# The first output tile inside the last attention block, and every gate in the blocks

## The chip, the cores and the metric

The kernel runs on one core of a Trainium2 chip. The metric is the device time of one execution in microseconds (us). The engines are named as in the profile: PE is TensorE (matmuls; PEld is its weight load), DVE VectorE, ACT ScalarE, POOL GpSimd, SP SyncE, whose queue issues the DMAs.

## What is computed

A backbone of two layers over 256 context and 2048 latent tokens, width 1024, in fp32. Each layer norms and projects its input once, runs four branches on the projection, multiplies each with SiLU of its own gate z, and projects the four branches together into the residual:

```python
for i in range(DEPTH):
    hl = rms_norm(xl, norm_g[i]) * (1.0 + sc_l[:, None]) + sh_l[:, None]
    (aq_l, ak_l, av_l, az_l, bq_l, bk_l, bv_l, bz_l, cu_l, cv_l, cz_l,
     dq_l, dk_l, dv_l, dz_l, drf_l, drb_l) = split_cols(hl @ w_in[i])
    ...
    y_l = jnp.concatenate([ya_l * jax.nn.silu(az_l), yb_l * jax.nn.silu(bz_l),
                           yc_l * jax.nn.silu(cz_l), yd_l * jax.nn.silu(dz_l)], axis=-1)
    xl = xl + gt_l[:, None] * (y_l @ w_out[i])
return rms_norm(xl, final_norm_g)
```

Branch A is differential attention (4 heads, two softmax maps each, the second subtracted with a learned weight), B grouped-query attention (4 query heads, 2 key heads), C a spatial-gating MLP over chunks of 128 tokens, D gated linear attention scanned in both directions. Latent tokens attend to context and latent tokens; context tokens, in layer 0 alone, to context only.

## The kernel before, in words

A layer has three stages. `proj_attn` and `proj_cd` norm the input, project it for the four branches and run C and D; the normed input goes to DRAM as `hs`, since the gates are projected later. `attention` runs A and B. `output` gates, turns and projects the branches.

**Attention** (L783) has four rounds, one per head, of eight blocks of 256 queries against all 2304 keys, from the last queries to the first; in layer 0 one block of the 256 context queries stands ahead of each round. PE's order is written out by hand: `Slots` (`S.at(slot, function, priority)`) collects calls and runs them slot by slot, by priority within one. A block has 18 slots: 12 score chunks of branch A (`da_chunk`, L893, read by DVE at L898), 6 of branch B for the row maxima (`g_chunk`, L931, L936). The two query transposes (`qb`, L945) close them. After that come, while the next block's chunks run, nine times four transposes of branch A's weights (`tr`, L953, copied by ACT, L957), nine times four score matmuls of branch B turned round (`gs`, L965 and L966, exp on ACT at L968, summed on POOL at L974), the products with V in 64-column tiles (`pvm`, L985) in four groups of 2, 2, 2 and 3 steps, and the output's turn and store (`o1` to `o3`, L992 to L1014). ACT takes the exps of branch A (L907), DVE joins the two maps (`da_comb`, L923). Only PE's order is fixed; a scheduler orders the other engines by data, buffers and the order of writing.

**The gates** (`gates`, L1142) are 24 matmuls for each of 4 groups and each token tile: 72 units in layer 0 (1728 matmuls), 64 in layer 1 (1536). They read `hs` back in halves of 512 KB (`fh`, three buffers), the weights `fw`, and go over PSUM bank `pz` and ACT (L1149) to DRAM as `z`. `Pace.fill` pours them in, at two calls per slot: `EARLY` puts more of them first, and `keep` holds back `HEAD` = 10 units for the start of the output. The last block's tail (its work after its query transposes, with no next block beside it) has `TAIL` = 22 slots of calls.

**The output** (`output`, L1161) goes over the token tiles. For each it steps the backward state of D's scan (`scan`: load of `bst` L1199, steps on DVE L1208, expansion to `SXb` on POOL L494), loads the branches and z (`load`, L1221 to L1225), gates and norms them (`mixers`: Silu L1231, state product `pd` L1235, Square L1242 and the inverse root L166, L167 with a table load, L152), transposes the tile (`turned`: L1257, copied by ACT and DVE) and projects it in two halves of 512 columns (`project`: 24 matmuls L139 to L141 into `po`). Each half of the output weights is loaded in eight pieces (L124) over four `wst` buffers and split into a high and a low part by ACT (L127, L130) and DVE (L128, L131). At the start the kept gates stand between these steps (`pace.units`).

## Time and profile before

| | |
|---|---|
| median of three runs | 4014.12 us (4008.24 to 4018.21) |
| profiled execution, its time | 4011.71 us |
| its span | 4009.9 us |
| mean granted PE clock | 0.974 |
| PE busy | 3724.8 us (93%) in 25908 matmuls |
| weight loads on PE (PEld) | 3068.2 us (77%) |
| DVE / ACT / POOL busy | 2706.0 / 2200.6 / 1182.5 us |

Busy PE time is the time covered by matmul records; neighbouring records overlap, since matmuls are pipelined. A stage is cut out of the span by its first and last instruction: layer 0's attention starts at 667.6 us and layer 1's at 2667.6; the block intervals begin with the first full block's `qb` and end with the last one's; the tail is the last block's rest, and the head lasts from there to the first output matmul (L139).

### The profile page before, as it was taken

How to read it: one execution, taken by the hardware profiler on the slowest of the kernel's cores; microseconds unless marked ns; L12 is line 12 of the kernel's file. 1: busy time of each engine (PE TensorE's matmuls, PEld its weight loads, DVE VectorE, ACT ScalarE, POOL GpSimd, SP SyncE). 2: the span in 40 equal slices, each digit the busy share in tenths (PEclk: the TensorE clock that was granted, in tenths of full speed). 3: DMA queues.
4: the chain of work that ended last, by engine and by line, in shares of the span. 5: the costliest groups of instructions: out<-in, count | busy, mean ns of one | idle time of the engine just before them, and what ended most of it. 6: DMA issues, size and time to landing. Idle time of an engine off the chain costs nothing.

```text
span 4009.9 us, 71922 instructions
## 1 busy us (share of the span) xinstructions
PE 3724.8 (93%) x25908; PEld 3068.2 (77%) x25908; DVE 2706.0 (67%) x6272; ACT 2200.6 (55%) x4527; POOL 1182.5 (29%) x1326
## 2 busy tenths in 40 slices
PE   7999997899999999978989999979999999999698
PEld 5888886787887877767778878867777777777576
DVE  5654443788888888854556544448888888886476
ACT  4433443666666666653444334436676666666464
POOL 1223221233333333332321222213333333334132
PEclk8999998999999999989999999989999999999899
DMA  7654434524234233246556542244242332322743
GB/s 271 194 184 161 147 125 144 157 83 128 86 100 131 85 102 94 86 151 232 177 181 213 170 149 88 89 144 129 80 124 81 114 95 80 99 87 71 249 165 120
DMA packets 407524, 537.73 MB, mean 134 GB/s; under 512 B 107832, under 2 KB 271616, under 8 KB 407168
## 3 DMA queue, kind: packets, MB, share of 16 engines
q1 hardware_dynamic: 407168, 533.14, 41.8%
q8 instruction: 205, 3.36, 0.3%
q14 instruction: 151, 1.24, 0.1%
HBM read 395.63 MB, written 137.32 MB: 133 GB/s over the span
## 4 chain that ended last, share of the span: by engine, by line
PE 34%; DVE 11%; DMA 4%; issue 3%; ACT 2%; POOL 1%; SPq 1%; DVEq 0%; POOLq 0%; ACTq 0%
PE pv L985 4%; DVE e L923 3%; PE pz L1142 3%; DVE junk L936 3%; PE s L893 2%; PE po L139 2%; DVE e L898 2%; PE po L141 2%; PE po L140 2%; PE b L953 2%; DMA fh<-hs 2%; PE s L931 1%; PE b L966 1%; PE b L965 1%; PE pc L139 1%
## 5 line engine op out<-in xcount | busy, mean ns | idle before, releaser
L974 POOL TENSOR_TENSOR acc<-acc,gp 128x512 f32<-128x512 f32 x448 | 591.2, 1320 | 1030.6 <-ACT gp L968 1026.9
L1142 PE MATMUL pz<-fw,fh 128*128 128x256 f32 x3264 | 726.0, 307 | 91.6 <-DMA fh<-hs 70.7
L907 ACT ACTIVATE e<-e,dm 128x1152 f32<-128x1152 f32 x512 | 640.5, 1254 | 17.5 <-DVE e L898 16.7
L1142 PEld LDWEIGHTS pz<-fw,fh 128*128 128x128 f32 x3264 | 543.6, 199 | 108.6 <-issue 34.5
L985 PE MATMUL pv<-gp,v 128*64 128x256 f32 x2320 | 558.4, 386 | 0.0
L985 PE MATMUL pv<-wt,v 128*64 128x256 f32 x2320 | 558.4, 385 | 0.0
L898 DVE TENSOR_SCALAR_CACHE_REDUCE e<-s,dm 128x768 f32<-128x768 f32 x512 | 511.3, 1013 | 47.0 <-PE s L893 41.2
L957 ACT COPY wt<-b 128x512 f32<-128x512 f32 x580 | 338.2, 583 | 364.0 <-PE b L953 361.5
L893 PE MATMUL s<-dak,daq 128*128 128x384 f32 (+1 forms) x1568 | 417.8, 348 | 58.7 <-DVE e L898 34.8
L968 ACT ACTIVATE gp<-b 128x512 f32<-128x512 f32 x580 | 346.2, 597 | 226.5 <-PE b L966 217.8
L923 DVE SCALAR_TENSOR_TENSOR e<-e,r,e 128x576 f32<-128x576 f32 x512 | 459.6, 934 | 2.7
L985 PEld LDWEIGHTS pv<-gp,v 128*64 128x64 f32 x2320 | 296.8, 137 | 162.2 <-issue 13.5
L953 PE MATMUL b<-ident,e 128*128 128x128 f32 x2304 | 360.4, 279 | 9.1 <-ACT wt L957 2.9
L898 DVE TENSOR_SCALAR_CACHE_REDUCE e<-s 128x768 f32<-128x768 f32 x256 | 239.8, 951 | 186.2 <-PE s L893 182.4
L953 PEld LDWEIGHTS b<-ident,e 128*128 128x128 f32 x2304 | 261.2, 140 | 106.3 <-issue 70.4
L936 DVE TENSOR_SCALAR_CACHE_REDUCE junk<-s,gm 128x768 bf16<-128x768 f32 x256 | 259.6, 1014 | 80.2 <-PE s L931 69.6
L965 PE MATMUL b<-qa,ka 128*128 128x256 f32 x1160 | 304.4, 285 | 7.2 <-ACT gp L968 5.5
L893 PEld LDWEIGHTS s<-dak,daq 128*128 128x128 f32 x1568 | 245.6, 193 | 79.5 <-DVE e L898 50.2
L966 PE MATMUL b<-qb,kb 128*128 128x256 f32 x1160 | 301.5, 282 | 0.0
L985 PEld LDWEIGHTS pv<-wt,v 128*64 128x64 f32 x2320 | 296.5, 137 | 0.0
L931 PE MATMUL s<-ka,qa 128*128 128x384 f32 (+1 forms) x784 | 219.0, 360 | 31.0 <-DVE e L898 20.7
L965 PEld LDWEIGHTS b<-qa,ka 128*128 128x128 f32 x1160 | 219.1, 189 | 13.7 <-ACT gp L968 10.8
(276 smaller groups left out, 8087.8 us busy)
## 6 DMA issues: line engine op xcount, KB each, us to landing
fh<-hs SPq DMA_DIRECT2D x272, 512.0 KB
hs<-hh SPq DMA_DIRECT2D x36, 512.0 KB
hs<-hl SPq DMA_DIRECT2D x36, 512.0 KB
hh<-hs SPq DMA_DIRECT2D x36, 512.0 KB
hl<-hs SPq DMA_DIRECT2D x36, 512.0 KB
dak<-aqk SPq DMA_DIRECT2D x96, 192.0 KB
daq<-aqk SPq DMA_DIRECT2D x136, 128.0 KB
z<-zs SPq DMA_DIRECT2D x136, 128.0 KB
```

What stands on the lines that cost most here:

```text
L893: nc.tensor.matmul(s[:, u, :hc], lhsT=Q["daq"][m][:, qt * P : (qt + 1) * P], rhs=R["dak"][m][c][:, u * hc : (u + 1) * hc], start=True, sto ...
L898: nc.vector.tensor_scalar(out=E[qt, m][:, c * ch : (c + 1) * ch].rearrange("p (u f) -> p u f", u=2), in0=s[:, :, :hc], scalar1=-SC, scalar ...
L907: nc.scalar.activation(e, e, AF.Exp, bias=NM[qt, m], scale=-1.0, accum_out=L[qt][:, b, m : m + 1])
L923: nc.vector.scalar_tensor_tensor(out=E0[:, a : a + w], in0=E1[:, a : a + w], scalar=RR[qt][:, 3:4], in1=E0[:, a : a + w], op0=ALU.mult, op ...
L936: nc.vector.tensor_scalar(out=junk[:, :ch].rearrange("p (u f) -> p u f", u=2), in0=s[:, :, :hc], scalar1=-1.0, scalar2=GM.get(qt, BIG), op ...
L953: nc.tensor.transpose(s[:, j * 256 + qt * P : j * 256 + (qt + 1) * P], W[qt][:, k * P : (k + 1) * P], ident)
L965: nc.tensor.matmul(o, lhsT=R["KA"][k // 6][:, ks], rhs=Q["QA"], start=True, stop=False)
L966: nc.tensor.matmul(o, lhsT=R["KB"][k // 6][:, ks], rhs=Q["QB"], start=False, stop=True)
L968: nc.scalar.activation(g, s, AF.Exp, scale=0.125)
L974: nc.gpsimd.tensor_tensor(out=B["acc"], in0=B["acc"], in1=g, op=ALU.add)
L985: nc.tensor.matmul(B["pv"][o : o + 64, :256], lhsT=R["V"][k // VH][:, k % VH, o : o + 64], rhs=x[:, js], start=k == 0, stop=k == nkt - 1,)
L1142: nc.tensor.matmul(ps[:, :256], lhsT=h[:, a, k % 4], rhs=w[:, b], start=k == 0 and z == 0, stop=k == KT - 1 and z == 2)
```

## The change

**The gates** are spread evenly over the calls of the 32 blocks, `EARLY`, `HEAD` and the tail's calls are gone; what is left after the last block's calls is drained before the tail. The first four slots take none.

**The output** becomes a generator whose first part runs as steps in the tail of the last block: at slot 2 the state, the first tile's loads and the first half of the output weights (eight pieces into the free buffers of branch A's weights, `room`), at slot 9 `mixers`, at slot 19 `turned`, from slot 20.5 eight steps of three output matmuls into the gates' bank. PSUM and SBUF tiles for it are lent by attention (`front`). After attention come the second tile's load and scan, the second half of the weights, and the steps tile by tile.

**Context blocks** are laid beside the first full block of a round, a chunk every second slot, with query and row buffers of their own and one exp of 256 in place of two of 128. In layer 0's first round the first full block's query is loaded first, then all keys of branch A, and the context's query after the first keys of branch B and the gates' first weights.

**V products** come in three groups of three steps, a slot earlier after their last step; `da_comb` gets slots of its own.

```diff
-EARLY, HEAD = 1.5, 10
...
-        w = lambda z: z + EARLY * min(z, 40)
-        want = (self.n - self.keep) * min(1, w(self.seen) / w(self.calls))
+        want = self.n * self.seen / self.calls
...
-    def units(self, n):
-        for _ in range(n):
-            while self.step():
-                pass
+    def drain(self):
+        for _ in self.steps:
+            pass
...
+        if isinstance(stage, bass.AP):
+            st = stage
+        else:
+            pool, tag, bufs = stage or (self.xp, "wst", self.wst)
+            st = pool.tile([P, 512 if stage is None else w], F32, name=tag, tag=tag, bufs=bufs)
...
-                gate = self.attention(i)
+                out = self.output(i)
+                self.attention(i, out)
                 self.xp, self.wst = dense.enter_context(self.pool(f"dn{i}", 2)), 4
-                ahead = self.output(i, *gate)
+                for _ in out:
+                    pass
+                ahead = self.ahead
...
+                ctx = "c" if q0 == 0 else ""
+                bufs = 1 if q0 == 0 else 3
...
-                    w = nk // 2
+                    w = nk // 2 if full else nk
...
-                s = base
+
+                s, step = (base, 1) if full else (base + 0.25, 2)
+                combs = ((11, 12, 14, 16.5), (17.5, 19, 21, 22.5))
                 for qt in range(2):
                     for c in range(nch):
                         for m in range(2):
                             S.at(s, lambda qt=qt, m=m, c=c: da_chunk(qt, m, c), 7)
-                            s += 1 if full else 0.5
+                            s += step
                     for m in range(2):
-                        for b in range(2):
+                        for b in range(2 if full else 1):
                             S.at(s + 1 + 2 * m + b, lambda qt=qt, m=m, b=b: da_exp(qt, m, b), -1)
                     npt = 4 if full else 1
                     for p in range(npt):
-                        S.at(s + 5 + p, lambda qt=qt, p=p: da_comb(qt, p, npt), 0.5)
+                        S.at(base + combs[qt][p] if full else s + 5, lambda qt=qt, p=p: da_comb(qt, p, npt), 0.5)
                 for c in range(nch):
                     for qt in range(2):
                         S.at(s, lambda qt=qt, c=c: g_chunk(qt, c), 0)
-                        s += 1 if full else 0.5
-                S.at(s + full, qb, 8 if full else 2)
-                for z in range(int(base), int(s) + (TAIL if (h, q0) == (3, NCTX) else 0)):
-                    S.at(z, lambda z=z: pace.fill(z), 3)
-                    S.at(z, lambda z=z: pace.fill(z + 0.5), 9)
+                        s += step
...
+                S.at(s + 1, qb, 8)
                 b0 = s + 2
                 if full:
+                    for z in range(base, s):
+                        S.at(z, lambda z=z: pace.fill(z), 3)
+                        S.at(z, lambda z=z: pace.fill(z + 0.5), 9)
                     for u in range(nu):
                         S.at(b0 + 2 * u, lambda u=u: tr(u), 1)
                         S.at(b0 + 2 * u + 1, lambda u=u: gs(u), 4)
-                    for us in ((0, 1), (2, 3), (4, 5), (6, 7, 8)):
+                    for us in ((0, 1, 2), (3, 4, 5), (6, 7, 8)):
+                        e = b0 + 2 * us[-1] + 4.5
                         for u in us:
                             for j in range(2):
-                                S.at(b0 + 2 * us[-1] + 5.5, lambda u=u, j=j: pvm(u, j), 5)
-                    e = b0 + 2 * (nu - 1) + 5.5
+                                S.at(e, lambda u=u, j=j: pvm(u, j), 5)
                 else:
-                    S.at(b0 + 20, lambda: tr(0), 3)
-                    S.at(b0 + 20, lambda: gs(0), 4)
+
+                    e = base + 24.25
+                    S.at(e - 3, lambda: tr(0), 3)
+                    S.at(e - 3, lambda: gs(0), 4)
                     for j in range(2):
-                        S.at(b0 + 20 + 1.5 + j * 0.5, lambda j=j: pvm(0, j), 5)
-                    e = b0 + 20 + 1.5 + 0.5
+                        S.at(e, lambda j=j: pvm(0, j), 5)
                 S.at(e, o1, 5.5)
                 S.at(e + 4, o2, 5)
                 S.at(e + 4, o3, 5.2)
                 return s
...
-            blocks = []
-            for r in range(4):
-                if with_ctx:
-                    blocks.append((r, 0, NCTX))
-                for b in reversed(range(8)):
-                    blocks.append((r, NCTX + 256 * b, NT))
+            blocks = [(r, NCTX + 256 * b) for r in range(4) for b in reversed(range(8))]
             units = 4 * (NTILE if with_ctx else NTILE - CTILE)
-            pace = Pace(self.gates(i, fp, pz), 24 * units, 2 * (32 * 18 + with_ctx * 12 + TAIL), 24 * HEAD)
+            pace = Pace(self.gates(i, fp, pz), 24 * units, 2 * 32 * 18)
             base = 0
             R = new_round(0, None)
-            ld_dak(R, 0)
             Qs = {0: qload(R, blocks[0][1])}
-            if with_ctx:
-                ld_ka(R, 0)
-                Qs[1] = qload(R, blocks[1][1])
+            for c in range(NCH):
+                ld_dak(R, c)
+            ld_ka(R, 0)
+            pace.begin()
             for c in range(1, NCH):
-                ld_dak(R, c)
-            pace.begin()
-            for c in range(with_ctx, NCH):
                 ld_ka(R, c)
             for c in range(2):
                 S.at(6 + 4 * c, lambda c=c, R=R: ld_v(R, c), 8)
-            for bi, (r, q0, nk) in enumerate(blocks):
-                end = block(R, Qs[bi], q0, nk, base)
+            for bi, (r, q0) in enumerate(blocks):
+                if with_ctx and bi % 8 == 0:
+                    block(R, qload(R, 0), 0, NCTX, base)
+                end = block(R, Qs[bi], q0, NT, base)
                 Rx = R
                 if bi + 1 < len(blocks):
                     if blocks[bi + 1][0] != r:
...
                     def pre(bi=bi, Rx=Rx):
                         Qs[bi + 1] = qload(Rx, blocks[bi + 1][1])
 
-                    if bi + 1 not in Qs:
-                        S.at(base + 1, pre, 8)
+                    S.at(base + 1, pre, 8)
...
+            pace.drain()
             dcx.close()
+            zcx.close()
+
+            S.run(base + 2)
+            self.front = dict(
+                pcx=pcx,
+                psum=lambda: pf.tile([P, 2, 512], F32, name="s", tag="s"),
+                bank=lambda: pz.tile([P, 512], F32, name="pz", tag="pz"),
+                room=[ep.tile([P, NT], F32, name=n, tag=n, bufs=b) for n, b in (("e0", 4), ("e0", 4), ("e1", 2))],
+                junk=lambda: tp.tile([P, 512], F32, name="wt", tag="wt", bufs=6),
+            )
+            for slot in (2, 9, 19) + tuple(20.5 + 0.5 * z for z in range(8)):
+                S.at(base + slot, lambda: next(out), 6)
             S.run()
-        return pace, zcx, pcx
...
-                y = self.xp.tile([P, DM], F32, name="xa", tag="xa", bufs=3)
+                if front:
+                    y, z = front["room"][0][:, 0:DM], front["room"][0][:, DM : 2 * DM]
+                else:
+                    y = self.xp.tile([P, DM], F32, name="xa", tag="xa", bufs=3)
+                    z = sp.tile([P, DM], F32, name="zt", tag="zt", bufs=3)
...
+            SX = states()
             bsts = [scan(t) for t in order[: order.index(outs[0]) + 1]][-1:]
-            T = [load(t) for t in outs[:2]]
-            Wo = []
-            for b in range(2):
-                Wo += self.weights(wo[b], f"o{b}", [512])
-                self.out_weights(i, Wo[b], b, gcol)
+            T = [load(outs[0])]
+            Wo = self.weights(wcx.enter_context(self.pool(f"ow{i}a", 1, side="right")), "oa", [512])
+            st = [r[:, j * 512 : (j + 1) * 512] for r in front["room"][1:] for j in range(4)]
+            self.out_weights(i, Wo[0], 0, gcol, st)
+            yield
+            mixers(bsts[0], T[0])
+            yield
+            turned(T[0])
+            yield
+            T[0]["po"] = front["bank"]()
+            for k in range(KT):
+                self.mm3(T[0]["po"], *T[0]["turn"], *Wo[0], 0, 512, [k])
+                yield
+            pcx, front = front["pcx"], None
+            cp = cx.enter_context(self.pool(f"oc{i}", 1))
+            xp = cx.enter_context(self.pool(f"ox{i}", 2))
+            sp = cx.enter_context(self.pool(f"os{i}", 2))
+            wo = cx.enter_context(self.pool(f"ow{i}b", 1))
+            pt = cx.enter_context(self.pool(f"opt{i}", 2, PSUM))
+            pg = cx.enter_context(self.pool(f"og{i}", 2, PSUM))
+            if last:
+                fg = cp.tile([P, DM], F32, name="fg")
+                nc.sync.dma_start(out=fg, in_=rows_bc(I["final_norm_g"], P))
+                nc.vector.tensor_scalar(out=fg, in0=fg, scalar1=32.0, scalar2=None, op0=ALU.mult)
+            SX = states()
+            T.append(load(outs[1]))
+            bsts.append(scan(outs[1]))
+            Wo += self.weights(wo, "ob", [512])
+            self.out_weights(i, Wo[1], 1, gcol)
...
-            steps = [(0, 0), (1, 0), (0, 1), (1, 1)]
             tail = 0 if last else 2
-            steps += [(n, b) for n in range(2, NO - tail) for b in range(2)]
+            steps = [(n, b) for n in range(NO - tail) for b in range(2)]
             if tail:
                 steps += [(NO - 2, 0), (NO - 1, 0), (NO - 2, 1), (NO - 1, 1)]
-            firsts = {n: k for k, (n, b) in enumerate(steps) if b == 0}
-            pace.units(2)
-            chain(0)
-            pace.units(HEAD - 4)
-            turned(T[0])
             chain(1)
-            pace.units(2)
-            chain(2)
-            pace.units(HEAD)
-            zcx.close()
             for k, (n, b) in enumerate(steps):
-                if k + 1 in firsts.values():
+                if n == 1 and b == 0:
+                    turned(T[1])
+                elif n and k + 1 < len(steps) and steps[k + 1][1] == 0:
                     turned(T[steps[k + 1][0]])
-                if b == 0 and n > 0:
+                if b == 0:
                     chain(n + 2)
                 project(T[n], b)
```

PE at the start of layer 0's attention. `s<-dak,daq` are score chunks (128x128 for the context, 128x384 for a full block; the number behind a name tells tiles apart), `pz<-fw,fh` gates. Before:

```order
L696 MATMUL po<-SX_3560,qe 32x256 x4
L1142 MATMUL pz<-fw,fh 128x256 x3
L893 MATMUL s<-dak_7492,daq_7498 128x128 x2
L1142 MATMUL pz<-fw,fh 128x256 x3
L893 MATMUL s<-dak_7495,daq_7500 128x128 x2
L1142 MATMUL pz<-fw,fh 128x256 x3
```

After:

```order
L699 MATMUL po<-SX_3560,qe 32x256 x4
L898 MATMUL s<-dak_7500,daq_7492 128x384 x2
L898 MATMUL s<-dak_7500,daq_7577 128x128 x2
L898 MATMUL s<-dak_7503,daq_7494 128x384 x2
L898 MATMUL s<-dak_7506,daq_7492 128x384 x2
L898 MATMUL s<-dak_7503,daq_7579 128x128 x2
L898 MATMUL s<-dak_7509,daq_7494 128x384 x2
L1158 MATMUL pz<-fw,fh 128x256 x5
```

The full block's chunks now lead, the context's stand second and fifth among them, and the first gates come behind six chunks.

ACT in the tail of layer 0's last block. `gp<-b` is an exp of branch B, `wt<-b` a copy of transposes, `oah` the high part of the first output weights, the `e` tiles the lent buffers. Before:

```order
L968 ACTIVATE gp<-b 128x512
L957 COPY wt<-b 128x512
L968 ACTIVATE gp<-b 128x512
L992 COPY ot<-pv 128x256
L957 COPY wt<-b 128x512
L968 ACTIVATE gp<-b 128x512
```

After:

```order
L974 ACTIVATE gp<-b 128x512
L127 CAST oah_20322<-e_20283 128x512 x2
L963 COPY wt<-b 128x512
L1245 ACT_TABLE_LOAD
L1245 ACTIVATE e_20281<-e_20281 128x1024
L130 ACTIVATE oah_20322<-e_20283,gcol 128x512 x2
L130 ACTIVATE oah_20322<-e_20282,gcol 128x512
L1000 COPY ot<-pv 128x256
L130 ACTIVATE oah_20322<-e_20282,gcol 128x512
L127 CAST oah_20322<-e_20282 128x512
L974 ACT_TABLE_LOAD
L974 ACTIVATE gp<-b 128x512
```

Two table loads, the first tile's Silu and six of the eight weight splits now stand between two exps of the last block.

PE from the end of layer 0's attention to the output. Before:

```order
L1142 MATMUL pz<-fw,fh 128x256 x21
L998 MATMUL b<-ident,ot 128x128
L999 MATMUL b<-ones,acc 128x2
L998 MATMUL b<-ident,ot 128x128
L999 MATMUL b<-ones,acc 128x2
L1142 MATMUL pz<-fw,fh 128x256 x3
L1235 MATMUL pd<-SXb,bst 32x256 x4
L1142 MATMUL pz<-fw,fh 128x256 x144
L1257 MATMUL py<-ident,xa 128x128 x8
L1235 MATMUL pd<-SXb,bst 32x256 x4
L1142 MATMUL pz<-fw,fh 128x256 x48
```

After:

```order
L139 MATMUL pz<-oah_20322,turnh 128x512
L140 MATMUL pz<-oal_20323,turnh 128x512
L141 MATMUL pz<-oah_20322,turnl 128x512
L1006 MATMUL b<-ident,ot 128x128
L1007 MATMUL b<-ones,acc 128x2
L1006 MATMUL b<-ident,ot 128x128
L1007 MATMUL b<-ones,acc 128x2
L1249 MATMUL pd<-SXb,bst 32x256 x8
L139 MATMUL po<-obh_20667,turnh 128x512
```

The first tile's first half is done before the last block's output is turned, and the gates between attention and the projection are gone.

## Rows read from the trace of the kernel before

**Rows 1.** The page's PE row: the span in 40 slices, busy tenths.

```profile
PE   7999997899999999978989999979999999999698
```

**Rows 2.** Windows by stage: start, blocks, tail, head, first layer 0, then layer 1. Columns: window, us, busy us of each engine (x instructions), PE clock, DMA share, GB/s.

```profile
667.60:729.70 62.10, 33.52 (x178) 28.73 (x175) 29.92 (x76) 18.99 (x47) 0.00 (x0) 0.70 0.80 226
729.70:1736.20 1006.50, 960.90 (x7247) 793.84 (x7244) 836.73 (x1703) 677.32 (x1256) 354.22 (x283) 1.00 0.33 101
1736.20:1767.50 31.30, 30.63 (x255) 24.84 (x254) 5.32 (x13) 16.36 (x29) 16.38 (x18) 1.00 0.44 142
1767.50:1843.90 76.40, 39.31 (x257) 35.53 (x258) 27.17 (x65) 24.34 (x43) 6.68 (x15) 0.75 0.75 238
2667.60:2718.40 50.80, 28.57 (x141) 25.42 (x137) 27.04 (x57) 14.14 (x27) 0.00 (x0) 0.73 0.80 222
2718.40:3683.70 965.30, 923.12 (x6953) 762.80 (x6952) 818.18 (x1632) 657.30 (x1186) 351.45 (x279) 1.00 0.32 95
3683.70:3711.00 27.30, 26.89 (x225) 21.37 (x224) 2.36 (x5) 12.71 (x24) 14.55 (x13) 1.00 0.28 88
3711.00:3790.50 79.50, 43.79 (x284) 38.85 (x284) 31.65 (x81) 28.60 (x47) 8.05 (x22) 0.79 0.79 256
```

**Rows 3.** The chain of waits in layer 0's head: start, us, what the chain goes through.

```profile
1825.89 8.12 DMA fh<-hs
...
1843.02 0.87 PE py L1257 x8
1843.89 0.23 PE po L139
```

**Rows 4.** Windows of the gate matmuls alone (L1142): PE and PEld busy us (x).

```profile
729.70:1736.20 1006.50, 304.09 (x1320) 220.40 (x1320) 1.00 0.33 101
1736.20:1767.50 31.30, 12.59 (x72) 9.84 (x72) 1.00 0.44 142
2718.40:3683.70 965.30, 281.38 (x1158) 199.01 (x1158) 1.00 0.32 95
3683.70:3711.00 27.30, 9.32 (x46) 6.73 (x46) 1.00 0.28 88
1055.50:1181.10 125.60, 38.10 (x167) 27.81 (x167) 1.00 0.27 86
2807.90:2930.70 122.80, 35.66 (x146) 25.09 (x146) 1.00 0.32 96
1181.10:1285.10 104.00, 30.66 (x133) 22.30 (x133) 1.00 0.47 133
```

**Rows 5.** PE's timeline around one group of V products: start, us, instruction, count.

```profile
1732.56 0.28 PE L966 MATMUL b<-qb,kb 128*128 128x256 f32 x1
1732.68 0.28 PE L1142 MATMUL pz<-fw,fh 128*128 128x256 f32 x1
1732.89 0.43 PE L985 MATMUL pv<-gp,v 128*64 128x256 f32 x1
...
1734.45 0.38 PE L985 MATMUL pv<-gp,v 128*64 128x256 f32 x1
...
1734.77 0.65 PE L953 MATMUL b<-ident,e 128*128 128x128 f32 x4
```

**Rows 6.** PE's timeline in the heads of layer 0 and of layer 1.

```profile
1780.52 2.93 PE L1142 MATMUL pz<-fw,fh 128*128 128x256 f32 x12 [10.57 <-DMA fh<-hs]
...
3725.63 1.08 PE L1235 MATMUL pd<-SXb,bst 128*32 128x256 f32 x8 [11.50 <-POOL SXb L494]
```

**Rows 7.** ACT's timeline in tail and head of layer 0.

```profile
1762.91 1.28 ACT L1231 ACT_TABLE_LOAD   x1 [1.70 <-DMA zt<-z]
1764.20 1.06 ACT L1231 ACTIVATE zt<-zt 128x1024 f32<-128x1024 f32 x1
...
1777.45 1.34 ACT L130 ACTIVATE o0h<-wst,gcol 128x512 fp32r<-128x512 f32 x2 [2.62 <-DMA wst<-in_w_out_dram]
```

**Rows 8.** POOL's timeline in the head of layer 0.

```profile
1788.04 2.81 POOL L494 TENSOR_SCALAR SXb<-Sc 32x256 f32<-32x256 f32 x4 [21.30 <-DVE Sc L1208]
```

83 lines of the change are left out of this document (40 added, 43 removed).

## The prediction

> **What bounds the kernel now.** I read the slices of the page first: TensorE (PE) is full nearly everywhere, and what dips there are lie where one stage hands over to the next [rows 1]. The windows by stage then give the four places that matter, once per layer [rows 2]. In the 31 block intervals of layer 0 (from the first full block's query transposes, L945, to those of the last) PE is busy 960.90 of 1006.50 us, and in layer 1 923.12 of 965.30, both at full clock; no other engine comes near that. So there PE's work sets the time. Ahead of the blocks and behind them it doesn't: PE is busy 33.52 of 62.10 us in layer 0's start, and in the head of the output (from the last block's end to the first output matmul, L139) 39.31 of 76.40 us, at a granted clock of 0.75; layer 1 shows the same. The head is made of gate matmuls (L1142) that wait for their own loads, one of them 8.12 us in the chain of waits [rows 3], while the first output weights are loaded and split. The change takes work out of the badly used places and puts it into the full one. The question is what an added matmul costs in a block, and how much of the head really goes.
>
> **1. Start of attention.** No gate stands ahead of the first score chunks any more, and the context block lies among the first full block's. By the order of instructions 120 gates stood in layer 0's start, and 59 do after; in layer 1 96, and 48 after. PE idles 28.6 us of the 62.10, so fewer gates alone give little; what goes is the context block as a piece of its own, 8.8 us (part 4). I take −9 for layer 0 and −2 for layer 1, where only the order of loads changes: **−11**. Bounds: −20 (the start of layer 0 as short as that of layer 1, 50.8 against 62.1, and some in both) and +5, since the context query is loaded behind all keys and two score chunks wait for it on PE, with everything behind them.
>
> **2. Gates into the blocks.** Counted by the order of instructions, 1669 gate matmuls stand in layer 0's block intervals after, and 1488 in layer 1's; before they were 1320 and 1158 [rows 4]. Extra: 349+330 = 679. Their price comes from two stretches of four like blocks: 167 gates in 125.60 us in layer 0, 146 in 122.80 in layer 1 [rows 4]. (125.60−122.80)/(167−146) = 0.133 us each, little over the 0.12 from one matmul's start to the next [rows 5]. 679×0.133 = **+90.3**. The stretches show 37 to 42 gates per block, and the change wants 48 to 54, so this goes beyond what is seen. Bounds: PE's idle time in the blocks, 45.6+42.2 = 87.8 us, swallows all but 2; and 0.16 us each gives 109. A higher price is a rival below.
>
> What hides their loads: a unit's 1 MB takes part of the DMA share, 0.33 here, and a third half-tile is in flight. Gates per block grow by a quarter; I cost it at nothing, and the load waits that the head shows (8.12 us at a DMA share of 0.75) would be the price if that cover went.
>
> **3. V products in three groups.** On either side of a group of 64-column matmuls PE loses a little [rows 5]: from the gate matmul to the first of the group 0.21 us, against 0.12 ahead of it; from the last to the transposes 0.32, against 0.22 within the group ((1734.45−1732.89)/7). 0.09+0.10 = 0.19 us for each group that goes, 62 in the block intervals: **−11.8**; bounds 0 (the gap falls on time in which the next buffer wasn't free anyway) and −17.
>
> **4. Context beside others (layer 0).** Three plain blocks and one with context took 104.00 us [rows 4]; 3×31.4 (125.60/4) and about 1 us for its gates leave 8.8. Its some 36 matmuls at 0.133 are 4.8 us of PE, the rest is its own chain of score, exp, combine and product. Beside other work the matmuls stay: −4.0 in each of three rounds, **−12** (the fourth is in part 1). Bounds 0 and −26.
>
> **5. The last block's end and the head.** From the last query transposes to the first output matmul it took 31.30+76.40 = 107.7 us, and 27.30+79.50 = 106.8 [rows 2].
> PE work left in the tail: 31.3−72×0.133 = 21.7, less one group 0.2; to it come the first tile's matmuls, the products with the scan's state (L1235, 0.54, half of the 1.08 that they take at half clock), eight transposes (0.87) and 24 of 0.23 us [rows 3, 6], together 6.9. That is 28.4 us, 27.9 in layer 1 (46 gates out).
> Waits that are new in the tail. ScalarE (ACT) gets, between the second and the third exp, two table loads of 1.28, Silu 1.06, six splits of 0.67 and a copy as long [rows 7], 8.3 us, and a load's wait like the 1.70 in those rows: 10.0. Behind them are queued the exps and the copies of transposes on ACT, and PE has two banks for them, so it stops. Square with its table load 2.0, the copies of the turned tile 2.0. PE's matmuls after such stops run at half clock, as at 1780.52, 12 gates in 2.93 us or 0.244 each [rows 6]; on 7 us of work that is 3.5 more. Sum 17.5. In layer 1 three dependent state loads with one buffer, and the expansion on GpSimd (POOL) at 2.81 [rows 8] queued behind the sums of the exps there, add 4: 21.5.
> Then the valley. The second half of the weights is loaded only when the attention's buffers are free: 2 MB at 238 GB/s, the rate of this stage [rows 2], are 8.8 us; PE has meanwhile the products of the state for the next tile (1.08) and then the first tile's second 24 matmuls (5.6). 15.5 together.
> So 28.4+17.5+15.5 = 61.4, and 27.9+21.5+15.5 = 64.9. At their end 48 output matmuls are done (11.0), less the next tile's transposes of 0.87 that before had behind it: 10.1 ahead. Saved: 107.7−51.3 = 56.4 and 106.8−54.8 = 52.0, **−108.4**. The weakest terms are the waits, 56.6 us in all: if they are half as long it is −137, if they double −52.
> On the SP queue the first tile's and the weights' loads now wait for buffers freed in the last blocks; behind them stand only the last stores of attention, for which nobody in the tail waits, so I cost that at nothing.
>
> The Silu in the rows starts at 1764.20, 0.01 us after the end of its 1.28 us table load [rows 7]: no pause shows. The Trainium skill ("ScalarE: Activation LUTs", What ACT_TABLE_LOAD costs) gives the load 1283 ns and a drain of some 1380 ns more; the trace agrees with the first figure and shows nothing of the second. By the page, three switches in each tail would make the sum an estimated 8.3 us worse.
>
> **Sum** against the profiled execution's 4011.7 us (span 4009.9): −11+90.3−11.8−12−108.4 = **−52.9**, 3958.8. The median of the runs is 4014.1, so 4014.1−52.9 = **3961**.
>
> **Rivals.**
> *Gates absorbed.* PE's records cover 95% of the block intervals, but a record overlaps its neighbour (0.28 us long, 0.12 us apart [rows 5]), and the weight loads fill 793.84 of 1006.50, 79%. If the added matmuls fall into the 87.8 us of idle time, part 2 costs 2.5: 4014.1−52.9−87.8 = 3873, and 3917 if half of it does. Against it: the slope of 0.133 comes from blocks that had the same idle time. The Trainium skill ("Perfetto Trace Analysis", Identifying the Most-Contended Engine) says that matmul busy time is no measure of how near PE is to its limit and that the busy share of weight loads is; by that rule room is left, and this is the case.
> *The head doesn't go.* The first tile's chain stalls ACT's in-order queue so that the waits of part 5 double: the head's idle time has only moved into the tail. −51.8 in place of −108.4: 4014.1−52.9+56.6 = 4018, no change. For it: three table switches in the tail, and the half clock that follows an idle PE. Against: ACT is busy only 16.36 of the tail's 31.30 us [rows 2].
> *Slower: the dense blocks pay a gate's whole length.* In the blocks the recorded busy time of a gate is 304.09/1320 = 0.230 us [rows 4]. If, with three to a slot, the weight loads no longer overlap and each added one takes that, part 2 is 679×0.230 = 156.2 and the time 4014.1−52.9+65.9 = 4027. It decides from 0.133+52.9/679 = 0.211 us each. Against it: starts 0.12 us apart in the same blocks.
>
> **How the numbers follow.** Chances: the forecast (3925 to 3997) 0.66, gates absorbed (below 3925) 0.11, the head doesn't go (around 4018) 0.12, dense blocks 0.11. A measurement here tells 0.3%, 12 us, from no change. Faster by more than that (below 4002): 0.66+0.11 and a little of the third, 0.78; within 0.3%: the rest of it, 0.11; slower 0.11. The range leaves out the fourth case and most of the second: 3908 to 4020.
>
> **What would show it.** The block intervals of layer 0 should grow by 349×0.133−5.9−12 = +29 us to about 1035 and layer 1's by 330×0.133−5.9 = +38 to about 1003; more than 1060 and 1030 means the dense blocks, under 1000 and 965 the absorbed gates. The last query transposes to the first output matmul of weight half two should fall to about 56 us (the 61.4 less 5.6), at a PE idle share of nearly half; 80 would mean that the head only moved. ACT's rows between the second and third exp of the last block should show 10 us without one, PE's first matmuls behind it the half clock. Layer 0's start should be near 53 us. The forecast is wrong if a wait appears in every block, as from a gate load or a combine that comes late: 64 blocks times 1 us would undo it.

## The result, and the profile after

The changed kernel takes 3956.62 us (median, 3953.0 to 3957.84), the kernel before 4016.16 (4008.24 to 4019.71): a ratio of 0.9853, 95% interval 0.9836 to 0.9870. The prediction was 3961 with a range of 3908 to 4020. The profiled execution took 3955.55, its span 3953.7, 56.2 less than before.

The windows of the changed kernel by stage, in the order of [rows 2]: start, blocks, tail to the first tile's first output matmul, and from there to the first matmul of the second weight half (the valley of the prediction), layer 0, then layer 1. Columns: window, us, busy us of PE, PEld, DVE, ACT, POOL (x instructions), PE clock, DMA share, GB/s.

```profile
667.00:720.60 53.60, 23.76 (x121) 19.35 (x114) 27.30 (x70) 16.46 (x34) 0.00 (x0) 0.68 0.68 185
720.60:1750.40 1029.80, 994.35 (x7595) 843.43 (x7592) 820.04 (x1701) 681.16 (x1247) 346.97 (x283) 0.99 0.38 115
1750.40:1784.00 33.60, 24.36 (x168) 17.24 (x168) 12.02 (x29) 21.97 (x37) 17.40 (x18) 0.84 0.26 77
1784.00:1800.20 16.20, 12.41 (x73) 8.22 (x71) 7.07 (x17) 9.14 (x11) 6.13 (x13) 0.82 0.73 239
2630.00:2674.00 44.00, 24.89 (x92) 20.39 (x89) 24.13 (x53) 13.48 (x25) 0.00 (x0) 0.61 0.76 202
2674.00:3667.00 993.00, 951.39 (x7285) 810.75 (x7283) 793.06 (x1638) 665.63 (x1200) 342.46 (x279) 0.99 0.36 108
3667.00:3707.00 40.00, 26.12 (x167) 17.91 (x168) 15.51 (x37) 22.13 (x37) 16.97 (x20) 0.79 0.27 81
3707.00:3731.80 24.80, 11.47 (x74) 7.18 (x71) 11.40 (x24) 10.61 (x16) 7.42 (x13) 0.74 0.58 185
```

For all kernels the span was cut at the same PE instructions: the start runs from the last matmul of `proj_cd` to the first full block's query transposes, the rest from the last block's query transposes to the last matmul ahead of the next attention (in layer 1 to the end). Each kernel's span is the sum of these and some 667 us ahead of layer 0's start, in us:

| kernel | start 0 | blocks 0 | rest 0 | start 1 | blocks 1 | rest 1 | median of the runs |
|---|---|---|---|---|---|---|---|
| before | 62.6 | 1006.4 | 930.9 | 51.3 | 965.3 | 326.2 | 4010 to 4016 |
| changed | 53.7 | 1029.8 | 879.1 | 44.5 | 992.9 | 286.7 | 3956.6 |
| e1_v3 | 61.8 | 988.4 | 927.2 | 50.6 | 955.4 | 327.3 | 3981.4 |
| e2_gates | 49.2 | 1035.5 | 882.0 | 41.0 | 988.4 | 287.4 | 3952.8 |
| e3_ctx | 53.0 | 1035.6 | 877.6 | 44.3 | 991.3 | 287.1 | 3958.8 |
| e4_o2 | 52.8 | 1023.6 | 875.4 | 44.0 | 980.0 | 286.4 | 3933.3 |
| e5_phase | 55.5 | 1022.5 | 875.6 | 45.5 | 987.0 | 279.2 | 3930.8 |
| e6_states | 53.3 | 1026.6 | 877.7 | 44.4 | 994.9 | 285.7 | 3950.7 |
| e8_silu | 52.2 | 1031.0 | 880.4 | 43.6 | 993.1 | 289.9 | 3957.3 |
| e9_nofront | 49.0 | 1010.9 | 884.1 | 40.6 | 979.8 | 291.3 | 3925.6 |
| r1_all | 51.9 | 1023.1 | 875.7 | 43.3 | 973.7 | 277.3 | 3912.7 |
| r2_ctx | 54.3 | 1022.0 | 873.1 | 45.2 | 972.4 | 277.5 | 3914.5 |
| r3_nofront | 56.1 | 1024.9 | 881.7 | 45.8 | 976.1 | 291.0 | 3943.8 |

Against before the changed kernel wins 8.9 and 6.8 us in the starts, pays 23.4 and 27.6 in the blocks, and wins 51.8 and 39.5 in the rests.

Each row of the table is one execution. e6_states and e8_silu, whose edits leave the blocks alone, differ from the changed kernel by up to 3.2 us in one stage, so a few us there tell nothing. The medians come from four sets of runs, with a kernel before of 4016.2 us for the changed kernel, 4010.8 for e1, e2, e3 and e5, 4011.9 for e4, e6, e8 and e9, and 4010.0 for the r runs; across sets, 6 us tell nothing either.

### The profile page after: what moved, and what is told of

Same layout as the page of the kernel before. It is cut to its first block, busy times and chain, and to the rows that moved or that the text cites. A ratio compares the mean times of both kernels' runs of the same rounds, so it can differ in the third digit from the quotient of the medians.

```text
span 3953.7 us, 71741 instructions
## 1 busy us (share of the span) xinstructions
PE 3705.2 (94%) x25908; PEld 3077.9 (78%) x25908; DVE 2669.6 (68%) x6264; ACT 2216.3 (56%) x4508; POOL 1175.1 (30%) x1328
## 4 chain that ended last, share of the span: by engine, by line
PE 75%; DVE 8%; DMA 6%; ACT 5%; issue 3%; SPq 1%; POOL 1%; DVEq 0%; ACTq 0%; POOLq 0%
PE pv L993 12%; PE pz L1158 8%; PE b L959 6%; PE s L898 5%; PE b L971 4%; PE s L937 3%; PE b L972 3%; PE po L139 2%; PE po L141 2%; PE po L140 2%; DVE e L903 2%; PE pc L139 2%; PE pc L140 2%; PE pc L141 2%; DVE e L929 1%
## 5 line engine op out<-in xcount | busy, mean ns | idle before, releaser
L982 POOL TENSOR_TENSOR acc<-acc,gp 128x512 f32<-128x512 f32 x448 | 578.6, 1292 | 955.2 <-ACT gp L974 946.9
L1158 PE MATMUL pz<-fw,fh 128*128 128x256 f32 x3264 | 710.9, 303 | 9.6 <-DMA fh<-hs 5.5
L1158 PEld LDWEIGHTS pz<-fw,fh 128*128 128x128 f32 x3264 | 528.1, 193 | 53.3 <-issue 44.9
L993 PE MATMUL pv<-wt,v 128*64 128x256 f32 x2320 | 548.3, 386 | 0.0
L993 PE MATMUL pv<-gp,v 128*64 128x256 f32 x2320 | 548.3, 386 | 0.0
L974 ACT ACTIVATE gp<-b 128x512 f32<-128x512 f32 x580 | 345.9, 596 | 359.4 <-PE b L972 344.4
L898 PE MATMUL s<-dak,daq 128*128 128x384 f32 x1568 | 420.6, 350 | 43.0 <-DMA daq<-aqk 17.9
L929 DVE SCALAR_TENSOR_TENSOR e<-e,r,e 128x576 f32<-128x576 f32 x512 | 397.1, 826 | 3.4
L971 PE MATMUL b<-qa,ka 128*128 128x256 f32 x1160 | 317.1, 295 | 52.8 <-ACT gp L974 28.5
L959 PEld LDWEIGHTS b<-ident,e 128*128 128x128 f32 x2304 | 274.2, 142 | 33.0 <-ACT gp L974 11.9
L971 PEld LDWEIGHTS b<-qa,ka 128*128 128x128 f32 x1160 | 220.4, 190 | 77.7 <-ACT gp L974 37.2
```

The lines of the kernel that those rows point to most:

```text
L898: nc.tensor.matmul(s[:, u, :hc], lhsT=Q["daq"][m][:, qt * P : (qt + 1) * P], rhs=R["dak"][m][c][:, u * hc : (u + 1) * hc], start=True, sto ...
L929: nc.vector.scalar_tensor_tensor(out=E0[:, a : a + w], in0=E1[:, a : a + w], scalar=RR[qt][:, 3:4], in1=E0[:, a : a + w], op0=ALU.mult, op ...
L959: nc.tensor.transpose(s[:, j * 256 + qt * P : j * 256 + (qt + 1) * P], W[qt][:, k * P : (k + 1) * P], ident)
L971: nc.tensor.matmul(o, lhsT=R["KA"][k // 6][:, ks], rhs=Q["QA"], start=True, stop=False)
L974: nc.scalar.activation(g, s, AF.Exp, scale=0.125)
L982: nc.gpsimd.tensor_tensor(out=B["acc"], in0=B["acc"], in1=g, op=ALU.add)
```

## Experiments

### One part alone: V groups, gates

**e1_v3**, three V groups in the kernel before:

```diff
-                    for us in ((0, 1), (2, 3), (4, 5), (6, 7, 8)):
+                    for us in ((0, 1, 2), (3, 4, 5), (6, 7, 8)):
+                        e = b0 + 2 * us[-1] + 4.5
...
-                                S.at(b0 + 2 * us[-1] + 5.5, lambda u=u, j=j: pvm(u, j), 5)
-                    e = b0 + 2 * (nu - 1) + 5.5
+                                S.at(e, lambda u=u, j=j: pvm(u, j), 5)
```

> The kernel before with one edit: V products in three groups of three, a slot earlier. After the change a plain block of layer 1 takes 31.2 us with 48 gates, before 30.7 with 37. Theory 1, a gate costs the forecast 0.133 us: then the three groups must have paid for the rest, 30.7+11x0.133-31.2 = 0.96 us per block, and this kernel is 62x0.96 = 60 us faster than before, 3956. Theory 2, a group change costs the forecast 0.19 us and gates are cheap: 62x0.19 = 12 us faster, about 4004.

Measured 3981.36 (ratio 0.9935, 0.9920 to 0.9950), about 29 us faster, between the two theories. 18.1 and 9.9 us come from the blocks, 0.45 per block. So the edit is worth more than 0.19 us per block, but not enough for a gate at 0.133. It also sets every group and the output's turn a slot earlier, so the 0.45 isn't the price of a group alone.

**e2_gates**, even gates in the kernel before and nothing else:

```diff
-EARLY, HEAD = 1.5, 10
+EARLY, HEAD = 0, 0
...
-            pace.units(2)
+            pace.units(72)
             chain(0)
-            pace.units(HEAD - 4)
```

> The kernel before with one edit: every gate inside the attention's slots, evenly spread, none kept for tail and head; no first tile in the tail. By the order of instructions 1661 and 1488 gates then stand in the block intervals, 671 more than before. In the blocks: theory 1 (0.133 us each) +89 us, theory 2 (about 0.06 each, from the plain blocks after the change) +40. The tails lose 118 gates, -16. Head: theory A, its length came from loads, splits and table switches that stay, so 50 us or more of the 76 to 80 remain and the first tile in the tail is what brings the gain: 4033 by theory 1, 3984 by theory 2. Theory B, the gates themselves with their loads made the head: about 22 us remain of each (2 MB of weights at 238 GB/s, 8.8 us, a split and the state's expansion), 3977 by theory 1 and 3928 by theory 2, which is faster than the whole change.

Measured 3952.75 (0.9860, 0.9845 to 0.9875): this part alone brings what the whole change brings (0.9853). Its windows, layer 0's blocks, tail with head, then layer 1's:

```profile
715.60:1751.10 1035.50, 998.73 (x7586) 842.49 (x7584) 837.90 (x1705) 684.91 (x1272) 352.37 (x283) 0.99 0.37 113
1751.10:1810.10 59.00, 30.44 (x223) 20.08 (x223) 25.15 (x63) 34.37 (x55) 21.88 (x28) 0.72 0.50 159
2674.10:3662.60 988.50, 954.54 (x7284) 807.29 (x7282) 846.93 (x1637) 660.52 (x1201) 358.04 (x279) 0.99 0.35 108
3662.60:3728.80 66.20, 30.13 (x223) 20.18 (x223) 29.33 (x76) 34.83 (x55) 22.48 (x33) 0.70 0.49 162
```

Tail and head fall from 107.7 and 106.8 us to 59.0 and 66.2 without any tile in the tail. Less the tail's own 21 to 22 us of PE work, 37 and 45 of each head remain, between theory A (50) and B (22). The gates with their load waits made about half of the head: PE waited 35.9 and 23.0 us for gate inputs in tail and head before. What is left are above all waits for the state's expansion on POOL (11.8 and 25.2 us) and for DVE's gating of the first tiles (12.4 and 5.9). The 671 added gates cost 29.1+23.1 = 52.2 us of blocks, 0.078 us each.

### The price of a gate, and a stall of the even spread

**e5_phase**:

```diff
-            pace = Pace(self.gates(i, fp, pz), 24 * units, 2 * 32 * 18)
+            pace = Pace(self.gates(i, fp, pz), 24 * units, 2 * 28 * 18)
```

> The changed kernel with one number altered: the gates are spread over 28 of the 32 blocks, so the change of gate weights falls one, two and three blocks ahead of the rounds' ends and not upon them, and the last four blocks of each layer have no gate at all. Theory: the new stall of 4 to 5 us at each end of a round (ScalarE waits up to 7.7 us for gate weights that are queued behind the next round's loads) is a coincidence of the even spread; it goes, 3 x 4 us per layer or about 22 us in all, 3935. Rival: the wait belongs to the weights' change wherever it falls: 3957. The blocks without gates against those with 62 give the price of a gate by themselves: 31.9-62x0.133 = 23.7 us for an empty block by the forecast's price, about 28 by 0.06.

Measured 3930.79 (0.9802, 0.9785 to 0.9819), 26 us below the changed kernel, as the theory says, though not at the place alone that it names: 13 us come from the blocks and 11 from the rests. The last blocks have no gates any more, and layer 1's tail is 32.3 us long in place of 40.1; which of the waits there that removes was not looked for. ACT's waits for gate weights in layer 0's blocks (columns: us in all, times, longest), the changed kernel, then e5_phase; before they were 5.8 us, the longest 4.0:

```profile
ACT fw L127 <- DMA fs<-in_w_in_dram: 22.7, 3, 7.7
```

```profile
ACT fw L127 <- DMA fs<-in_w_in_dram: 18.5, 15, 2.4
```

The sum hardly falls; what goes is the long single wait. ACT's timeline of the changed kernel at the end of the first round shows what hung behind it:

```profile
937.74 0.71 ACT L127 CAST fw<-fs 128x256 fp32r<-128x256 f32 x2
945.98 0.41 ACT L127 CAST fw<-fs 128x256 fp32r<-128x256 f32 x1 [7.52 <-DMA fs<-in_w_in_dram]
946.29 0.59 ACT L974 ACTIVATE gp<-b 128x512 f32<-128x512 f32 x1
```

The exp (L974) stands behind the split in ACT's queue, and PE needs it to free a bank. PE's waits for such exps in layer 0's blocks, the changed kernel, then e5_phase:

```profile
PE b L971 <- ACT gp L974: 12.0, 4, 4.2
```

```profile
PE b L971 <- ACT gp L974: 0.8, 3, 0.3
```

So waits of ACT of up to 2.4 us hardly reach PE there, and one of 7.5 does. In layer 1 the long waits stand ahead of the query transposes (L951, 8.8 us in two) and go as well, while those for exps rise from 3.0 to 6.6 us. 18 (layer 0) or 16 units per gate group, spread evenly over 32 blocks, make the change of weights fall upon each round's end. That the weights come late there because the next round's loads are ahead of them on the SP queue is argued from the order on the queue; that moving the change away from the round's end removes the long wait is what the run shows.

The last four blocks of each layer, without a gate, give the price of one within a layer. Four plain blocks (no context and no round's end beside them) of e5_phase's layer 1 with gates and the last four of the same layer without, each cut at the query transposes, then the 219 gates of the first:

```profile
2694.90:2822.20 127.30, 125.46 (x973) 106.90 (x972) 102.11 (x210) 85.86 (x154) 44.21 (x37) 1.00 0.35 113
3539.50:3651.80 112.30, 104.14 (x750) 78.67 (x749) 100.69 (x223) 84.27 (x148) 48.28 (x45) 1.00 0.10 28
```

```profile
2694.90:2822.20 127.30, 46.24 (x219) 34.02 (x219) 1.00 0.35 113
```

15.0 us for 219 gates are 0.069 us each (by the same cut 0.060 in r1_all, further below), though two gates start 0.12 apart at best. An empty block isn't full of PE work: in the last four PE idles 8.2 of 112.3 us, 4.9 of them in waits for DVE, which is busy 100.69, and 2.4 in waits for ACT. With the gates it idles 1.8. So 6.3 us of the gates' time fell into idle time. That the 219 gates add only 21.3 us to PE's busy time, 0.097 each and not 0.12, these runs leave open.

### Where the V groups' gain went

**e4_o2**:

```diff
-                S.at(e + 4, o2, 5)
-                S.at(e + 4, o3, 5.2)
+                S.at(e + 6, o2, 5)
+                S.at(e + 6, o3, 5.2)
```

> The changed kernel with one edit: the turn of a block's output (o2, o3) two slots later, so that it stands right ahead of a group of V products, as it did before the change. In the trace after, the matmul behind o2 is a score matmul of branch B in all 31 blocks of layer 1 and starts 0.91 us later than o2's last one (0.11 to 0.18 before the change): three users of two PSUM banks in a row, the third waits for ScalarE's copy. Theory: this wait is where the gain of three V groups went; it goes, 31 x 0.8 = 25 us in layer 1 and about 1 in layer 0, 3931. Rival: ScalarE or the banks are the limit there and the wait shows up at the next user: 3957.

PE's timeline in a plain block of the changed kernel's layer 1. Behind the output's turn (L1006, L1007) a score matmul of branch B (L971) needs a bank and waits for ACT's copy:

```profile
2779.16 0.27 PE L1006 MATMUL b<-ident,ot 128*128 128x128 f32 x1
2779.26 0.28 PE L1007 MATMUL b<-ones,acc 128*128 128x2 f32 x2
2779.41 0.31 PE L1006 MATMUL b<-ident,ot 128*128 128x128 f32 x1
2779.55 0.28 PE L1007 MATMUL b<-ones,acc 128*128 128x2 f32 x2
2780.57 0.38 PE L971 MATMUL b<-qa,ka 128*128 128x256 f32 x1 [0.73 <-ACT wt L963]
```

Measured 3933.33 (0.9804, 0.9788 to 0.9821), 23 us less, nearly the 25 expected, but only 12.9 of them in layer 1's blocks, where a plain block falls from 31.2 to 30.8 and not by 0.8. PE's waits there (us, times, longest), changed kernel and e4_o2:

```profile
PE b L971 <- ACT wt L963: 20.5, 29, 0.7
```

```profile
PE b L959 <- ACT wt L963: 11.7, 27, 0.6
```

Half of the wait has gone to the next user of the banks, as the rival says. Layer 0's blocks gain 6.2 and its rest 3.7, which the theory didn't foresee; what did it there was not looked for. Of what the V groups bring alone, 28 us in the blocks, the change kept little: against e2_gates its blocks are 5.7 us shorter in layer 0, where the context moved too, and 4.5 longer in layer 1.

### The tail

**e6_states**, with the loads for layer 1's states in another order:

```diff
-                bst = sp.tile([P, 388], F32, name="bst", tag="bst", bufs=1 if front else 3 if last else 2)
+                bst = sp.tile([P, 388], F32, name="bst", tag="bst", bufs=3 if last else 1 if front else 2)
...
-            T.append(load(outs[1]))
             bsts.append(scan(outs[1]))
+            T.append(load(outs[1]))
```

(The final norm's load moves behind the second half of the weights as well.)

> The changed kernel with the order of layer 1's output loads altered: three buffers for the state loads of its first tile, the second tile's state loaded ahead of its inputs, and the final norm's weights loaded last instead of first. Theory: layer 1's tail and head are 14 us longer than layer 0's (72.5 against 58.2 us to the end of the first tile's 48 matmuls) since PE waits 5.9 us in the tail for POOL's expansion behind state loads that come one at a time, and 8.2 and 5.5 us behind the tail for states whose loads stand on the SP queue behind the attention's last store: 12 to 15 us, 3942 to 3945. Rival: the output weights, which stand behind the same store, set the end anyway: 6 us or less, from the tail alone.

Measured 3950.70 (0.9844, 0.9829 to 0.9859). Layer 1's rest is 285.7 us against 286.7, so the theory fell. PE's waits in layer 1's tail and head (us, times, longest), changed kernel, then e6_states:

```profile
PE pd L1249 <- POOL SXb L497: 13.3, 2, 8.2
PE b L971 <- ACT gp L974: 6.3, 4, 5.4
PE s L1249 <- POOL SXb L497: 5.5, 1, 5.5
```

```profile
PE pd L1249 <- POOL SXb L497: 17.1, 1, 17.1
PE b L971 <- ACT gp L974: 4.3, 4, 3.4
...
PE s L1249 <- POOL SXb L497: 1.9, 1, 1.9
```

The tail's wait went (5.5 to 1.9), the one behind the tail grew from 13.3 to 17.1, and the output matmul started 65.4 us after the last query transposes, against 64.8 in the changed kernel. The weights' loads are issued right behind the store of the last block (3718.52 and 3717.08 us on the SP queue of the changed kernel), as the rival says. But they don't set the end alone. The chain of waits of e6_states up to the output matmul (L139):

```profile
3715.56 4.37 DMA wst<-in_w_out_dram
...
3724.38 0.66 DVE obl L131
3725.05 0.21 DVE Sc L1219
...
3727.13 0.41 POOL SXb L497
3727.59 1.08 PE pd L1249 x8
3728.67 0.73 PE po L139
```

It goes from a load of the weights to their split on DVE (L131), then to the third tile's state: its steps (L1219) stand behind the splits in DVE's queue, then come its expansion on POOL and its product on PE, which PE's written order puts ahead of the first tile's second half. The last split ends at 3725.0 us, the output matmul starts at 3728.6. To move the weights ahead of the store, or that product behind the second half, wasn't tried.

**e8_silu**:

```diff
-                B["silu"] = nc.scalar.activation(z, z, AF.Silu)
+                    B["silu"] = nc.scalar.activation(w, z, AF.Exp, scale=-1.0)
+                    nc.vector.tensor_scalar(out=w, in0=w, scalar1=1.0, scalar2=None, op0=ALU.add)
+                    nc.vector.reciprocal(w, w)
+                    nc.vector.tensor_tensor(out=z, in0=z, in1=w, op=ALU.mult)
```

> The changed kernel with the first tile's Silu in the tail computed as z/(1+exp(-z)), with the exp that is loaded already and three steps on VectorE, so that two of the three table loads in each tail go. Theory: ScalarE's queue between the second and third exp of the last block holds PE for 6.6 and 5.7 us; without two loads of 1.28 us that is 2.6 us less, 5 us in all, 3951. If each switch also costs a pause that the rows don't show (the Trainium skill, ScalarE: Activation LUTs, gives about 1.4 us), another 5.5 us: 3946. Rival: the six weight splits stay there and VectorE's three steps lie on the chain to the tile's transposes: no change.

Measured 3957.30 (0.9865, 0.9850 to 0.9880), no change. PE's waits in layer 0's tail, changed kernel, then e8_silu, and a row of DVE there:

```profile
PE b L971 <- ACT gp L974: 7.2, 4, 6.3
```

```profile
PE s L1257 <- POOL SXb L497: 8.8, 1, 8.8
PE b L971 <- ACT gp L974: 1.7, 4, 0.9
```

```profile
1759.30 6.55 DVE L1250 RECIPROCAL e<-e 128x1024 f32<-128x1024 f32 x1
```

ACT's hold went as hoped, 7.2 to 1.7 us. The reciprocal of 6.55 us took its place: the state's steps stood behind it on DVE, and PE waited 8.8 us for the state. So the rival was right. The time doesn't decide on a pause behind a table load, since the splits moved too.

**e9_nofront** is e2_gates with the two diffs of e1_v3 and e4_o2.

> The kernel before with the even gates, three V groups and the same later o2 as the run above, but without the first tile in the tail and with context blocks ahead of the rounds. Against the run above it tells what these two are worth. By the stage lengths of the runs so far (from the last query transposes to the next layer's start 882.0 and 287.4 us with the gates alone, 879.1 and 286.6 with the whole change) the tile in the tail is worth 4 us and the context 1 to 2: 5 us slower than the run above. Rival, the prediction's reading, in which the head would have kept its loads, splits and switches without the tile in the tail: half of the 108 us or more slower.

Measured 3925.59 (0.9785, 0.9770 to 0.9799), 8 us *faster* than e4_o2. The rests are longer without the tile in the tail, by 8.7 and 4.9 us, so the tile earns 13.5 there; starts and layer 0's blocks are shorter by 3.8, 3.4 and 12.7. So the rival fell far more clearly than the expectation, and something in the rest of the change costs about 20 us. Context blocks, the slots of `da_comb`, the order of first loads and the gates' rest at the start differ there together. Context blocks and loads are undone in e3_ctx and r2_ctx and the gates' rest in r1_all, each with little gain; the slots of `da_comb` were not tried by themselves.

### The parts put together

**r1_all** is the changed kernel with the diffs of e4_o2 and e5_phase and:

```diff
-        self.done, self.seen, self.rest = 0, 0, 4
+        self.done, self.seen, self.rest = 0, 0, 0
```

> The changed kernel with the two edits that helped (gates over 28 blocks, o2 ahead of a V group) and, as a third, no rest of four slots for the gates at the start of attention. Theory: the first two act at different places (ends of rounds, every block of layer 1) and add, 26+23 us; the start, 53.7 and 44.5 us after the change against 49.2 and 41.0 with the gates alone, loses 3 to 4 us per layer because of the rest: 3900 to 3908. Rival: the gates over 28 blocks already put a gate matmul behind o2 in two thirds of layer 1's blocks, so that o2's edit brings only 8 more, and the start depends on the order of loads: 3920.

Measured 3912.68 (0.9756, 0.9743 to 0.9770), faster than both kernels; between theory and rival. Of the 18 us below e5_phase 13.3 are in layer 1's blocks, where o2 acts, so it brought more than half of its 23 again; 5.7 are in the starts. Its tail with the valley takes 45.4 and 54.9 us, against 49.8 and 64.8 in the changed kernel. The starts are 51.9 and 43.3 us, 3.6 and 2.1 below e5_phase, its nearest partner, while o2's edit alone moved them by 0.9 and 0.5 (e4_o2). So the rest of four slots seems to cost 2 to 3 us in each start, a little less than the theory says. That they are still longer than the 49.2 and 41.0 of e2_gates goes along with the denser gates, which lengthen the start by 7.1 and 5.2 us in the kernel without the tile (r3_nofront against e9_nofront).

**r2_ctx** and **e3_ctx** set the context blocks ahead of the rounds again, in r1_all and in the changed kernel:

```diff
-                s, step = (base, 1) if full else (base + 0.25, 2)
+                s, step = (base, 1) if full else (base, 0.5)
...
-                    block(R, qload(R, 0), 0, NCTX, base)
+                    base = block(R, Qc or qload(R, 0), 0, NCTX, base)
+                    S.run(base)
```

> The changed kernel with one part undone: context blocks stand ahead of the rounds again, with the order of the first loads that belongs to it. Forecast: 4.0 us per round for three rounds and some 9 in the first one come back, 21 us, about 3977. Rival: the context's chain was hidden ahead of the rounds as well, and the start was shortened by the fewer gates: under 6 us, 3957 to 3962.

> The run above with the context blocks ahead of the rounds, as before the change. So far the context beside other work stood together with the change of gate weights at the end of a round, and the two cancelled: 1 us between them in the whole time. Forecast of 4.0 us per round, now without that stall: 8 to 12 us slower than the run above. Rival: its exps and combines on ScalarE and VectorE get in the way of the full block's, the same time or a few us faster.

Measured 3958.84 (0.9877, 0.9862 to 0.9891) and 3914.49 (0.9762, 0.9749 to 0.9776), each 2 us above its partner, no difference that can be told from none (e3_ctx and its partner are of different sets). In e3_ctx layer 0's blocks are 5.8 us longer, and the start is as short as the changed kernel's, 53.0 against 53.7.

**r3_nofront** is e9_nofront with the gates over 28 blocks.

> The run above without the first tile in the tail: the kernel before with three V groups, even gates over 28 blocks and the later o2. By the stages of the two runs that differ most nearly in it the tile in the tail saves 8.7 us in layer 0 and 4.8 in layer 1: 13 us slower than the run above. Rival: with no gates in the last four blocks the output's loads come early anyway and the tile in the tail only adds stops for ScalarE: the same time.

Measured 3943.79 (0.9836, 0.9822 to 0.9849), 29 us above r2_ctx: 8.6 and 13.4 in the rests, the remainder in starts and blocks. So with the gates out of the last blocks the tile in the tail is worth more in the rests, 22.0 us against 13.5, not less. The two kernels also differ in the slots of `da_comb`, so the 29 us aren't the tile's alone. Yet the same kernel with even gates (e9_nofront) takes 18 us less, with starts of 49.0 and 40.6 us against 56.1 and 45.8 and 14.0 us less in layer 0's blocks: denser gates cost without the tile and pay with it. Why, these runs leave open.

## Why the prediction was right, point by point

The time lay within 5 us of the forecast by luck: two errors of some 16 us cancel, and a third of 5 us is small.

| step | forecast | by stages |
|---|---|---|
| 1 start | −11 | −15.7 |
| 2 to 4 blocks: gates +90.3, V −11.8, context −12 | +66.5 | +51.0 |
| 5 tail and head | −108.4 | −91.3 |
| sum | −52.9 | −56.2 with −0.2 ahead of the starts |

The direction and its reason were right: gates that waited for their loads in a badly used head cost less inside the blocks. e2_gates shows this by itself.

**Bound.** Right: PE is busy 994.35 of 1029.80 us in the blocks after. But "no other engine comes near" hid what sets the price of a gate: in a block without gates DVE is busy 90% (100.69 of 112.30 us in e5_phase) beside PE's 93%, and PE's waits for DVE are idle time that gates can fill.

**Step 1.** Right in layer 0 (53.7, forecast 53), too small in layer 1 (−6.8, forecast −2). The reason was wrong: with the context apart (e3_ctx) the start is as short, and with nothing but even gates shorter (49.2, 41.0). It is the gates' going, which I had called worth little. What the prediction named as its upper bound did come: two score chunks wait for the context's query behind all keys, PE's longest wait in the changed kernel's start:

```profile
693.00 2.27 PE L898 MATMUL s<-dak,daq 128*128 128x128 f32 x6 [17.39 <-DMA daq<-aqk]
```

With the context apart PE waits as long for other loads there, 13.0 us for keys and 6.2 for gate inputs (e3_ctx).

**Step 2** is one of the two terms that failed in size. 0.133 us came from setting blocks of layer 0 against blocks of layer 1, which differ in more than their gates; measured within a layer it is 0.069 (e5_phase), and 0.078 with the new stall (e2_gates), so 679 gates cost 47 to 53 us and not 90. The gates in the blocks of the changed kernel, in the order of layers:

```profile
720.60:1750.40 1029.80, 352.90 (x1669) 262.57 (x1669) 0.99 0.38 115
2674.00:3667.00 993.00, 333.29 (x1488) 243.12 (x1488) 0.99 0.36 108
```

A gate's recorded length there is 0.21 and 0.22 us, against 0.23 and 0.24 in [rows 4], three times its price: the slower rival priced by it was out of reach. The rival of the absorbed gates was half right. The rule of the Trainium skill ("Perfetto Trace Analysis", Identifying the Most-Contended Engine), by which the share of weight loads shows the room, leans the right way: that share rose from 79% to 82% (843.43 of 1029.80) for a quarter more gates; but the room wasn't free.

"What hides their loads: ... I cost it at nothing" was right of the gates' inputs (PE waited 0.3 and 1.5 us for them in the blocks after) and wrong of their weights, which the step didn't weigh: the even spread set the change of weights upon the rounds' ends and cost some of what e5_phase got back.

**Step 3.** Alone the groups, set a slot earlier, bring 29 us, not 11.8; together with even gates the turn of the output fell between two users of the banks, and the gain was mostly gone. The prediction weighed an edit by its own gaps and didn't look at what then stood next to what.

**Step 4.** −12 and the −9 of step 1 were the context's; undone, it is 2 us (r2_ctx against r1_all).

**Step 5** is the other term that failed, behind the place where the prediction stopped counting. Up to that place it came out nearly as summed. ACT goes 10.3 us from the start of one exp to the next in layer 0 and 9.5 in layer 1 (forecast 10.0). ACT's timeline of the changed kernel there:

```profile
1752.38 0.60 ACT L974 ACTIVATE gp<-b 128x512 f32<-128x512 f32 x1
...
1754.51 1.28 ACT L1245 ACT_TABLE_LOAD   x1
1756.09 1.06 ACT L1245 ACTIVATE e<-e 128x1024 f32<-128x1024 f32 x1 [0.30 <-DMA e<-z]
...
1761.38 1.28 ACT L974 ACT_TABLE_LOAD   x1
1762.68 0.60 ACT L974 ACTIVATE gp<-b 128x512 f32<-128x512 f32 x1
```

Again no pause follows a table load (1761.38+1.28 to 1762.68), against the 1380 ns of the Trainium skill ("ScalarE: Activation LUTs", What ACT_TABLE_LOAD costs). From the last query transposes to the second half's first matmul it was 49.8 us in layer 0 and 64.8 in layer 1, forecast 55.8 and 59.3; layer 1's excess is the valley, 24.8 us against 16.2, where state and weights are loaded behind the last store.

With 24 output matmuls done, the changed kernel is there 63.9 and 48.0 us ahead of the kernel before (113.7 and 112.8 us behind the last query transposes), 111.9 together and more than the forecast of 108.4. The prediction then took the first tile's second 24 matmuls at full speed and put the tiles behind it at nothing. The next 72 output matmuls of layer 0, then the next 216 of layer 1, before:

```profile
1849.80:1868.00 18.20, 18.20 (x93) 14.51 (x89) 10.22 (x24) 10.44 (x12) 5.95 (x9) 1.00 0.73 242
3796.50:3853.50 57.00, 57.00 (x285) 44.26 (x281) 41.25 (x103) 39.40 (x57) 22.07 (x30) 1.00 0.48 161
```

In the changed kernel:

```profile
1800.20:1830.40 30.20, 25.19 (x108) 18.52 (x104) 22.68 (x60) 16.30 (x25) 8.64 (x14) 0.82 0.77 257
3731.80:3800.30 68.50, 63.41 (x301) 48.37 (x297) 52.53 (x141) 45.57 (x66) 24.48 (x35) 0.92 0.55 194
```

They take 12.0 and 11.5 us longer. PE idles 5.0 and 5.1 us, which are in layer 0 a wait for the fourth tile's state (2.9) and one for a turned tile (1.8), in layer 1 above all one for a turned tile (4.1). The granted clock is 0.82 and 0.92 where it was 1.00 before: in layer 0 it is 0.58 up to 1805 us, right behind a valley in which PE was busy 12.41 of 16.20 us, and 0.68 again behind those waits. And 15 and 16 more matmuls, transposes and state products, stand there, since the kernel before had prepared its next tiles in the head. 3 us come back later in layer 1. So part of the head's waiting moved behind the valley, where the prediction's sign (56 us, 80 if the head only moved) couldn't show it, and −108.4 became −91.3.

The credit belongs elsewhere, too: e2_gates has 48.9 and 38.7 us of this gain without the tile. At the 24th output matmul the changed kernel is 16.1 and 8.3 us ahead of e2_gates, and in the same stretches, which take 18.1 and 57.8 us there, it loses 12.1 and 10.7 of that. So the tile earned 3.6 of 91.3 in the changed kernel, and in the rests of other kernels 13.5 (e4_o2 against e9_nofront) and 22.0 (r2_ctx against r3_nofront).
